# Second mixer's projections in a fixed order, modulation chunks one per weight block and six of them in the attention

## The chip, the cores and the metric

One core of one Trainium2 chip runs the kernel. The metric is the device time of one execution in microseconds (us). TensorE does matrix products, VectorE and GpSimd elementwise work, ScalarE activation functions and copies; SyncE (SP) issues most of the DMA transfers. Each engine takes its instructions in the order in which the program lists them for it, and waits for others by semaphores.

## What is computed

A backbone of two layers. Each layer is a token mixer and a mixture of experts, both behind an RMS norm that is modulated by six vectors made from a condition `c`. Layer 0's mixer is a recurrence; layer 1's, which the change touches, is a bidirectional chunkwise mLSTM over 256 context and 512 latent tokens. Cut to that:

```python
def adaln(cond, w, b):
    m = jax.nn.silu(cond) @ w + b          # 1024 -> 6 * 1024
    return jnp.split(m, N_MOD, axis=-1)    # shift, scale, gate; shift, scale, gate

# layer 1
hx = modulate(rms_norm(x, g1), sh1, sc1)
p = hx @ w_in                              # q 512, k 512, v 1024, o 1024, gates 32 columns
...
w_intra = jnp.exp(log_w - m_t[..., None])
s = jnp.einsum('bhtd,bhsd->bhts', qc, kc) * w_intra
num = w_inter[..., None] * jnp.einsum('bhtd,bhde->bhte', qc, c_mat) + jnp.einsum('bhts,bhse->bhte', s, vc)
den = w_inter * jnp.einsum('bhtd,bhd->bht', qc, n_vec) + jnp.sum(s, axis=-1)
h_out = num / jnp.maximum(jnp.abs(den), jnp.exp(-m_t))[..., None]
...
y = (rms_norm_per_head(h_f + h_b) * sigmoid(o)) @ w_out
x = x + gt1 * y
x = x + gt2 * hier_moe(modulate(rms_norm(x, g2), sh2, sc2))
```

## The kernel before

Three stages of layer 1 matter here: the projections (`ml_in`), the attention (`ml_att`), and the product with `w_out` and the experts behind them.

**Projections.** `w_in` is taken in blocks of 256 columns. A block is loaded as fp32 (1 MB, tile `ws`, L1667) into a pool of three slots, and split into a high and a low part: ScalarE writes `whi` (L306), GpSimd `wlo` (L309), each in two halves of four k-tiles. A job is then one PSUM tile of 24 matmuls: eight k-tiles by three products of high and low parts. Blocks 0 and 1 are q, 2 and 3 are k, 4 to 7 are v, 8 to 11 are the output gate. q and k are made channel-major (`chan`, L1684, 512 tokens a matmul), k's context, v and the output gate token-major (`toks`, L1692, 256 columns a matmul). ScalarE copies each finished tile out of PSUM (qT L1755 and L1776, kT L1778, kc L1783, v L1789, og L1796). The PSUM pool `pa` of these tiles has two buffers. Block 0 and the gates are made ahead, during the norm.

**Modulation chunks.** Layer 1's modulation is 24 chunks of 256 columns, numbered n = 4 v + q for vector v and quarter q. Chunks 8 to 23 are made here, `ada_vec` (L194): a load of 1 MB into a slot of the same pool (L168), eight products on VectorE that sum over k-tiles with c as scalar (L202 the first, L204 seven more, tile `vpart`), and later a finish: two matmuls with ones (L210, four records in the trace), a VectorE add into `modT` (L214), a multiplication by the norm's weight where v is 1 or 4 (L218), and at q = 3 of v = 2, 3, 4 a transpose into a row (L227). Two chunks are begun in each of blocks 1 to 8 and finished at the end of the block after.

**Gates.** `ml_gates` makes the exponents of the chunkwise form: a chain on VectorE (L1819 to L1838, scans among it) with two activations between, then 18 exponentials on ScalarE (L1840 to L1848). `tokens`, called at block 3, transposes them. `ml_queries` (L1886), called at block 9, spreads the decays by matmuls (L1898) and weights q.

**What sets the order.** Ahead of this stretch the order is written out by hand. Within it a scheduler decides, instruction by instruction, from dependences and estimated times; the program order above is only its input. The attention is again in a hand-written order: eight steps, each with the scores and weights of the next step, states, and `values` of its own, two PSUM tiles `po` per step (`b0` 0 and 2). VectorE turns each tile into `hs` in six steps (L1993 to L2001). Behind the last transposes come the matmuls with `w_out` (L801), whose weights use the same three slots.

Of the kernel before, what the change touches and what calls it, by code (L numbers as in the profile page):

```python
# [17 lines left out]
P = 128  # L18
# [84 lines left out]
class Net:  # L103
# [90 lines left out]
    def ada_vec(self, l, n, pool, psum, work, tag="pg", m=2):  # L194


        V = self.nc.vector
        w = self.ada_load(l, n, pool)
        v, q = divmod(n, 4)
        part = work.tile([P, m, 256], F32, name="vpart", bufs=4 if m == 1 else 1)  # L200
        for i in range(m):
            V.tensor_scalar(part[:, i], w[:, 0, :], self.cT[:, 0, i:i + 1], None, op0=OP.mult)  # L202
            for k in range(1, KD):
                V.scalar_tensor_tensor(part[:, i], w[:, k, :], self.cT[:, k, i:i + 1], part[:, i],  # L204
                                       op0=OP.mult, op1=OP.add)
        def finish():
            ps = psum.tile([P, 512], F32, name=tag)
            for i in range(m):
                for b in range(2):
                    self.nc.tensor.matmul(ps[:, 2 * i + b:2 * i + b + 1], part[:, i, b * P:(b + 1) * P], self.ones,  # L210
                                          start=True, stop=True)
            ks = slice(2 * q, 2 * q + 2)
            o = self.modT[:, l, v, 0:m, ks]
            V.tensor_add(o, ps[:, 0:2 * m].rearrange("p (i b) -> p i b", b=2),  # L214
                         self.adab[l][:, v, ks].unsqueeze(1).to_broadcast([P, m, 2]))
            if v in (1, 4):
                g = (self.g1T if v == 1 else self.g2T)[l][:, ks]
                V.tensor_mul(o, o, g.unsqueeze(1).to_broadcast([P, m, 2]))  # L218
            if q == 3 and v >= 2 and (l, v) != (1, 5):
                self.ada_rows(l, v, ps[:, 256:512], work, m)  # L220
        return finish
# [1422 lines left out]
    def ml_in(self, x, xcp, wsp):  # L1644
# [4 lines left out]
        with ExitStack() as st:  # L1649
# [103 lines left out]
            nc.gpsimd.memset(self.v1[:, :, :, 128:129], 1.0)  # L1753
            for c in range(2):
                nc.scalar.activation(self.qT[:, c, :], psq[:, c * 512:(c + 1) * 512], AF.Copy, scale=0.125)  # L1755
            ps = psg
            for q in range(4):
                dst = (self.li, self.lf)[q % 2][32 * (q // 2):32 * (q // 2) + 32, :]
                nc.scalar.activation(dst, ps[32 * q:32 * q + 32, 256:1024], AF.Identity, bias=bg[32 * q:32 * q + 32, :])
            tokens = self.ml_gates(sp, gp, pb)  # L1760

            ada = []
            for i in range(12):
                parts = parts1 if i == 1 else split(load(256 * i, 256)) if i else None
                last, ada = ada, []
                if 1 <= i <= 8:
                    ada = [self.ada_vec(1, 6 + 2 * i + j, wsp, pb, sp, m=1) for j in range(2)]
                if i == 0:
                    pass
                elif i < 4:  # L1770
                    for c in range(2):
                        blk = 2 * (i % 2) + c
                        ps = pa.tile([P, 1024], F32, name="pa")[:, 0:512]
                        chan(ps, parts, c, CTX, NTOK)
                        if i < 2:
                            nc.scalar.activation(self.qT[:, blk, :], ps, AF.Copy, scale=0.125)  # L1776
                        else:
                            nc.scalar.activation(self.kT[:, blk, :], ps, AF.Copy)  # L1778
                    if i >= 2:
                        for t in range(2):  # L1780
                            ps = pa.tile([P, 1024], F32, name="pa")[:, 0:256]
                            toks(ps, parts, t)
                            nc.scalar.activation(self.kc[:, t, 256 * (i - 2):256 * (i - 1)], ps, AF.Copy)  # L1783
                elif i < 8:
                    for t in range(NT0):
                        ps = pa.tile([P, 1024], F32, name="pa")[:, 0:256]
                        toks(ps, parts, t)
                        h = 2 * (i - 4)
                        nc.scalar.activation(self.v1[:, t, h:h + 2, 0:128],  # L1789
                                             ps.rearrange("p (h e) -> p h e", e=128), AF.Copy)  # L1790
                else:
                    for t in range(4):
                        ps = pa.tile([P, 1024], F32, name="pa")[:, 0:256]
                        toks(ps, parts, 2 + t)
                        c = slice(256 * (i - 8), 256 * (i - 7))
                        nc.scalar.activation(self.og[:, t, c], ps, AF.Sigmoid)  # L1796
                if i == 3:
                    tokens()
                    gates.__exit__(None, None, None)
                if i == 7:  # L1800
                    hcp.__exit__(None, None, None)
                if i == 9:
                    self.ml_queries(store.enter_context(tc.tile_pool(name="queries", bufs=1)), pb)
                for f in last:
                    f()
        return store

    def ml_gates(self, sp, gp, psum):
# [31 lines left out]
        nc.scalar.activation(emn, m[:, CTX:NTOK], AF.Exp, scale=-1.0)  # L1840
        for d, (a, z) in enumerate(dirs):
            for c, (s, e) in enumerate(chunks):
                end = e - 1 if d == 0 else s
                if c > 0:
                    prev = s - 1 if d == 0 else (e if c < 4 else 0)
                    nc.scalar.activation(win[a:z, s - CTX:e - CTX], g[a:z, s:e], AF.Exp, bias=m[a:z, prev:prev + 1])
                if c == 0 or c != (4 if d == 0 else 1):
                    nc.scalar.activation(wst[a:z, s:e], r[a:z, s:e], AF.Exp, bias=g[a:z, end:end + 1])  # L1848
# [35 lines left out]
        return tokens  # L1884

    def ml_queries(self, pool, psum):  # L1886

        nc, V = self.nc, self.nc.vector
        self.qw = pool.tile([P, 2, 4, SEQ], F32, name="qw")
        self.dec = pool.tile([P, 2, 4, 4], F32, name="dec")  # L1890
        for d in range(2):
            for b in range(0, 4, 2):
                pw = psum.tile([P, 1024], F32, name="pg").rearrange("p (a n) -> p a n", a=2)
                for c in range(2):
                    sel = pool.tile([64, 2, 64], F32R, name="sel", bufs=2)
                    h = 2 * (b + c)
                    V.tensor_copy(sel, self.both[:, d, h:h + 2].bitcast(F32).unsqueeze(2).to_broadcast([64, 2, 64]))
                    nc.tensor.matmul(pw[:, c, :], sel.rearrange("p a b -> p (a b)"), self.wr, start=True, stop=True)  # L1898
                V.tensor_mul(self.qw[:, d, b:b + 2, :], self.qT[:, b:b + 2, :], pw)
                o = P - 1 if d == 0 else 0  # L1900
                V.tensor_copy(self.dec[:, d, b:b + 2, :], pw[:, :, o:512:P])

    def ml_att(self, st, yT):
# [69 lines left out]
        def weigh(c, h0, d):  # L1973
            V.tensor_mul(pds[c, h0][d], pds[c, h0][d], pss[c, h0])

        def values(i, between=None):
# [5 lines left out]
            for b0 in (0, 2):  # L1982
# [19 lines left out]
                if b0 == 0 and between:  # L2002
                    between()
# [44 lines left out]
        with tc.manual_schedule(engines={ET.PE, ET.DVE, ET.Activation, ET.Pool}):  # L2048
# [19 lines left out]
            for i in range(8):  # L2068
                nxt = steps[i + 1] if i < 7 else None
                if nxt:  # L2070
                    scores(*nxt)
                    weigh(*nxt, 0)
                if i < 3:
                    state(0, i + 1)
                if i:
                    squares(i - 1, G)
                    if i % 2 == 0:
                        roots(i // 2 - 1, 0, 8)
                    if i == 7:
                        roots(3, 0, 4)  # L2080
                if nxt:
                    weigh(*nxt, 1)
                values(i, (lambda: scale(3, 0, 4)) if i == 7 else None)
# [11 lines left out]
def body(tc, A, out, upto=None, dbg=None):  # L2095
    nc = tc.nc
    with ExitStack() as ctx:
# [34 lines left out]
        with ExitStack() as st:  # L2132
            n.ml_att(st, yT)
# [43 lines left out]
```

## Times and profile before

| what | us |
| --- | --- |
| three runs | 1878.0, 1901.58, 1873.12 |
| median | 1878.0 |
| profiled execution, its own time | 1875.53 |
| span of the profiled execution | 1873.5 |
| TensorE busy | 1736.0 (93%) |
| VectorE busy | 941.6 (50%) |
| ScalarE busy | 543.3 (29%) |
| GpSimd busy | 390.4 (21%) |

The profile is of one execution. Its page gives the busy time of every engine and the span in 40 equal slices; the trace can be asked for the busy time in any stretch, for what an engine waited for, and for the instructions one by one, with their start, duration and the idle time before them with what ended it. The mean granted TensorE clock of the execution is 0.964 of full speed. Neighbouring instructions of one kind are drawn together into one row with a count; matmuls are pipelined, so their durations overlap and the distance of starts tells the pace.

### The profile page before, as it was taken

The numbers are of one execution on the slowest core, as the hardware profiler recorded it, in microseconds if no ns is written. First come the engines' busy times: TensorE is split into PE (matmuls) and PEld (weight loads), VectorE is DVE, ScalarE is ACT, GpSimd is POOL, SyncE is SP. The second block draws the span as 40 slices with busy tenths as digits, with TensorE's granted clock in tenths as the row PEclk, the third lists the DMA queues.
The fourth block names the chain that finished last, engine by engine and source line by source line (L and its number), as shares of the span: only waits on it lengthen the run. The fifth ranks groups of instructions, "written<-read, shape, count | busy, mean of one in ns | idle before, by whom it ended". The sixth has DMA issues, their size and how long they took to land. (4 is left out here: it accounts for less than half of the span.)

```text
span 1873.5 us, 26159 instructions
## 1 busy us (share of the span) xinstructions
PE 1736.0 (93%) x10181; PEld 1038.1 (55%) x10181; DVE 941.6 (50%) x1877; ACT 543.3 (29%) x1007; POOL 390.4 (21%) x303
## 2 busy tenths in 40 slices
PE   7999998997999999999988998999978999999996
PEld 5777776685443434344447898977653444444342
DVE  5477776656444464545455743156552333333234
ACT  5367775422111110111126312145421111111112
POOL 3433322402111010101025242221221111111111
PEclk9999998998999999999999998999989999999999
DMA  9544432555999989999942545200869999999995
GB/s 331 178 157 149 126 120 90 177 174 227 416 419 418 371 315 419 418 419 419 418 161 80 180 135 164 84 1 1 311 244 418 421 421 420 420 420 420 420 421 222
DMA packets 158240, 521.13 MB, mean 278 GB/s; under 512 B 16744, under 2 KB 93806, under 8 KB 109984
## 3 DMA queue, kind: packets, MB, share of 16 engines
q1 hardware_dynamic: 151344, 497.08, 68.6%
q0 software_dynamic: 6768, 22.33, 3.0%
q8 instruction: 82, 1.34, 0.3%
q14 instruction: 46, 0.38, 0.1%
HBM read 518.59 MB, written 7.39 MB: 281 GB/s over the span
## 5 line engine op out<-in xcount | busy, mean ns | idle before, releaser
L1214 DVE TENSOR_TENSOR xl<-xl,ps 128x512 f32<-128x512 f32 x136 | 87.7, 684 | 296.6 <-PE ps L1212 296.6
L1198 POOL DMA_INDIRECT xg<-h_rows,idx x32 | 38.4, 1199 | 567.1 <-DVE slot L1181 257.1
L1276 PE MATMUL pd<-wring,hT 128*64 128x512 f32 (+1 forms) x616 | 152.1, 610 | 2.7 <-ACT hT L1268 2.1
L1251 PE MATMUL pu<-wring,xT 128*64 128x512 f32 (+1 forms) x576 | 149.1, 610 | 0.4 <-DMA wring<-in_l_moe_w_up_dram 0.4
L309 POOL TENSOR_TENSOR wlo<-ws,whi 128x1024 fp32r<-128x1024 f32 x41 | 114.4, 2800 | 119.6 <-ACT whi L306 118.1
L1239 POOL TENSOR_TENSOR yl<-yw,yh 128x512 fp32r<-128x512 f32 x60 | 76.4, 1273 | 248.7 <-ACT yh L1238 246.6
L1251 PE MATMUL pg<-wring,xT 128*64 128x512 f32 (+1 forms) x576 | 127.7, 594 | 0.0
L1258 ACT ACTIVATE sg<-pg 128x512 f32<-128x512 f32 x32 | 19.1, 597 | 351.0 <-PE pg L1251 351.0
L1692 PE MATMUL pa<-whi,hhi 128*128 128x256 f32 x352 | 103.6, 294 | 10.9 <-ACT v L1789 9.1
L1238 ACT ACTIVATE yh<-yw 128x512 fp32r<-128x512 f32 x64 | 40.3, 630 | 250.1 <-DVE yw L1235 127.5
L1230 DVE SCALAR_TENSOR_TENSOR yw<-pd,slotr,gt2b 128x512 f32<-128x512 f32 x62 | 46.5, 751 | 119.2 <-PE pd L1276 119.1
L1692 PE MATMUL pa<-whi,hlo 128*128 128x256 f32 x352 | 102.6, 292 | 0.0
L1692 PE MATMUL pa<-wlo,hhi 128*128 128x256 f32 x352 | 102.2, 290 | 0.0
L1251 PE MATMUL pu<-yt,xT 128*64 128x512 f32 (+1 forms) x408 | 95.6, 596 | 0.2 <-DMA yt<-in_l_moe_w_up_dram 0.2
L1276 PE MATMUL pd<-yt,hT 128*64 128x512 f32 (+1 forms) x376 | 86.9, 595 | 1.6 <-ACT hT L1268 1.1
L1207 ACT ACTIVATE xT<-tr 128x512 f32<-128x512 f32 x64 | 35.1, 595 | 179.5 <-PE tr L1206 179.5
L1276 PEld LDWEIGHTS pd<-wring,hT 128*64 128x64 f32 (+1 forms) x616 | 44.5, 133 | 75.3 <-issue 69.4
L1214 DVE TENSOR_TENSOR xl<-xl,pd 128x512 f32<-128x512 f32 x128 | 82.1, 680 | 0.3 <-PE pd L1212 0.3
L1251 PEld LDWEIGHTS pu<-wring,xT 128*64 128x64 f32 (+1 forms) x576 | 40.7, 133 | 73.8 <-issue 69.7
L1251 PE MATMUL pg<-yt,xT 128*64 128x512 f32 (+1 forms) x400 | 81.4, 596 | 0.0
L1212 PE MATMUL ps<-yh,oht 128*128 128x512 f32 x166 | 75.0, 452 | 5.9 <-DVEq L1355 5.9
L1251 PEld LDWEIGHTS pg<-wring,xT 128*64 128x64 f32 (+1 forms) x576 | 38.5, 131 | 70.9 <-issue 68.6
(628 smaller groups left out, 3924.8 us busy)
## 6 DMA issues: line engine op xcount, KB each, us to landing
wring<-in_l_moe_w_gate_dram SPq DMA_DIRECT2D x62, 1024.0 KB
wring<-in_l_moe_w_up_dram SPq DMA_DIRECT2D x61, 1024.0 KB
wring<-in_l_moe_w_down_dram SPq DMA_DIRECT2D x59, 1024.0 KB
yt<-in_l_moe_w_up_dram SPq DMA_DIRECT2D x41, 1024.0 KB
ws<-in_l_ada_w_dram SPq DMA_DIRECT2D x40, 1024.0 KB
yt<-in_l_moe_w_gate_dram SPq DMA_DIRECT2D x39, 1024.0 KB
yt<-in_l_moe_w_down_dram SPq DMA_DIRECT2D x35, 1024.0 KB
ws<-in_l_moe_w_gate_dram SPq DMA_DIRECT2D x24, 1024.0 KB
```

What stands on the lines that cost most here:

```text
L309: eng_lo.tensor_sub(lo, x, hi.bitcast(F32))
L1198: nc.gpsimd.indirect_dma_start(out=xg, out_offset=None, in_=hd, in_offset=bass.IndirectOffsetOnAxis(ap=idx[:, 0:1], axis=0), bounds_check= ...
L1207: nc.scalar.activation(xT[:, 4 * h:4 * h + 4, :], pt[:, :, 0:n], AF.Copy)
L1212: nc.tensor.matmul(ps, lhsT, y, start=i == 0, stop=i == len(ys) - 1)
L1214: V.tensor_add(xs, xs, ps)
L1230: V.scalar_tensor_tensor(y[k], ps, r[:, 1:2], g[:, 0, :], op0=OP.mult, op1=OP.mult)
L1238: nc.scalar.activation(yh, y, AF.Copy)
L1239: eng.tensor_sub(yl, y, yh.bitcast(F32))
L1251: nc.tensor.matmul(ps[a:a + w, :], xT[:, 4 * h + j, a:a + w], pieces[n, e[i], h][:, j, :], start=h == 0 and j == 0, stop=h == 1 and j == 3)
L1258: nc.scalar.activation(s, pg, AF.Silu)
L1276: nc.tensor.matmul(pd[a:a + w, :], hT[:, 2 * h + j, a:a + w], ring.down(2 * p + i, h, j, c), start=h == 0 and j == 0, stop=h == 1 and j == 1)
L1692: nc.tensor.matmul(ps, h, w[:, k % 4, :], start=k == 0 and j == 0, stop=k == KD - 1 and j == 2)
```

## The change

The whole stretch of the projections is put under a hand-written order, on SyncE too. Raw blocks are loaded two ahead; the next block's split is made in two halves ahead of a block's first two jobs; one chunk per block is begun in blocks 1 to 10 (chunks 8 to 17), its products behind the block's first job, its finish behind the first job of the block after. Chunks 18 to 23 go into the attention: their products are dealt out three, two and two at a time over the steps, a finish at the end of six steps, in free columns of the tile `po`. The exponentials are issued behind block 3's second job, `tokens` behind block 4's third, the queries in four pieces in blocks 9 and 10, with four `sel` tiles instead of two. qT's copies stand ahead of those of the gates.

```diff
@@ ada_vec becomes ada_prods (the eight products) and ada_fin
+        for b in range(2):
+            self.nc.tensor.matmul(ps[:, b:b + 1], part[:, b * P:(b + 1) * P], self.ones, start=True, stop=True)
+        ks = slice(2 * q, 2 * q + 2)
+        o = self.modT[:, l, v, 0, ks]
+        V.tensor_add(o, ps[:, 0:2], self.adab[l][:, v, ks])
+        if v in (1, 4):
+            V.tensor_mul(o, o, (self.g1T if v == 1 else self.g2T)[l][:, ks])
+        if q == 3 and v >= 2 and (l, v) != (1, 5):
+            self.ada_rows(l, v, ps[:, 8:136], work, 1)
@@ ml_in
+            st.enter_context(tc.manual_schedule(engines={ET.PE, ET.DVE, ET.Activation, ET.Pool, ET.SP}))
+            raws, ada, part = {2: load(512, 256)}, {}, {}
...
+            chunk(1)
+            fetch(3)
...
-            for i in range(12):
-                parts = parts1 if i == 1 else split(load(256 * i, 256)) if i else None
-                last, ada = ada, []
-                if 1 <= i <= 8:
-                    ada = [self.ada_vec(1, 6 + 2 * i + j, wsp, pb, sp, m=1) for j in range(2)]
...
+            for i in range(1, 12):
...
+                if i in ada:
+                    part[i] = sp.tile([P, 256], F32, name="vpart", bufs=2)
+                    prods = self.ada_prods(7 + i, ada.pop(i), part[i])
+                for j, job in enumerate(jobs):
+                    if j < 2 and i < 11:
+                        new += split(raws[i + 1], halves=(j,))
+                    job()
+                    if j == 0 and i - 1 in part:
+                        finish(i - 1)
+                    if j == 0:
+                        for f in prods:
+                            f()
+                        chunk(i + 1)
+                        fetch(i + 3)
+                    if i == 3 and j == 1:
+                        exps()
+                    if i == 4 and j == 2:
+                        tokens()
+                        gates.__exit__(None, None, None)
+                    if i == 8 and j == 1:
+                        queries = self.ml_queries(store.enter_context(tc.tile_pool(name="queries", bufs=1)), pb)
+                    if i in (9, 10) and j in (0, 2):
+                        queries.pop(0)()
...
+            self.chunks = [(n, self.ada_load(1, n, wsp)) for n in (18, 19, 20)]
@@ ml_att: behind each tile po; ada_some(3) and ada_some(2) also behind the two weighings of a step
-                if b0 == 0 and between:
-                    between()
+                if b0 == 0:
+                    ada_some(2)
+                    if between:
+                        between()
+                else:
+                    ada_end(po[:, 1, 376:512])
```

Three places of the order show what moves. The first is VectorE at the gates: L1819 to L1837 before are L1839 to L1857 after, and the products are L202 and L204 before, L199 and L201 after. Before, rows in their order:

```order
L1819 SCALAR_TENSOR_TENSOR og<-lf 64x768
L204 SCALAR_TENSOR_TENSOR vpart<-ws,cT,vpart 128x256 x6
L1821 TENSOR_SCALAR og<-og 64x768
L204 SCALAR_TENSOR_TENSOR vpart<-ws,cT,vpart 128x256 x3
L1823 SCALAR_TENSOR_TENSOR lf<-lf,og 64x768
L204 SCALAR_TENSOR_TENSOR vpart<-ws,cT,vpart 128x256
L1830 SCALAR_TENSOR_TENSOR og<-lf,li 32x768
```

After, the end of the same chain and what stands behind it (L212 is the add of a finish):

```order
L1856 TENSOR_TENSOR li<-li,og 64x768
L1857 TENSOR_TENSOR lf<-og 64x768
L1858 MEMSET og 64x768
L199 TENSOR_SCALAR vpart<-ws,cT 128x256
L201 SCALAR_TENSOR_TENSOR vpart<-ws,cT,vpart 128x256 x7
L212 TENSOR_TENSOR modT<-pg,svm_136 128x2
```

The products of a chunk stood between the gates' steps and now stand behind all of them. The second place is TensorE at the end of block 2's first job (L1679 is `chan` after the change, L209 a finish): here the finish of the first chunk stands.

```order
L1679 MATMUL pa<-hhi_8112,whi 128x512
L1679 MATMUL pa<-hlo_8113,whi 128x512
L1679 MATMUL pa<-hhi_8112,wlo 128x512
L209 MATMUL pg<-ones,vpart 128x1 x2
L1679 MATMUL pa<-hhi_8112,whi 128x512
```

Before, the first finish stood at the end of block 2, for two chunks at once, ahead of block 3's jobs:

```order
L1692 MATMUL pa<-whi,hhi_8110 128x256
L1692 MATMUL pa<-whi,hlo_8111 128x256
L1692 MATMUL pa<-wlo,hhi_8110 128x256
L210 MATMUL pg<-ones,vpart 128x1 x4
L1684 MATMUL pa<-hhi_8112,whi 128x512
```

It has moved forward by one channel job and two token jobs. The third place is TensorE in the attention behind the values of step 2 (counted from 0), where chunk 19 is finished (L209) and its row is transposed (L222), ahead of the next step's scores (L1994, L1998):

```order
L2028 MATMUL po<-v_8399,w_10383 128x129
L2029 MATMUL po<-C,qw 128x129
L209 MATMUL po<-ones,ws 128x1 x2
L222 MATMUL po<-ident,modT 8x128
L1994 LDWEIGHTS identb
L1994 MATMUL pw<-mask,identb 128x512
L1998 MATMUL pw<-gr,both 128x128 x4
```

Before the change the scores followed the values directly.

## Rows read from the trace of the kernel before

**Rows 1.** Busy by windows; columns as in the first line, clock in shares.
```profile
core 0: us, PE busy (x) PEld busy (x) DVE busy (x) ACT busy (x) POOL busy (x), PEclk, DMA share, GB/s
1023.90:1218.40 194.50, 179.42 (x1289) 169.60 (x1289) 88.28 (x197) 51.54 (x93) 56.93 (x21) 0.96 0.44 141
1218.40:1308.20 89.80, 88.69 (x596) 65.50 (x595) 54.17 (x158) 44.91 (x155) 16.91 (x14) 1.00 0.00 1
1500.00:1600.00 100.00, 97.71 (x490) 40.85 (x489) 33.57 (x74) 14.51 (x31) 15.93 (x12) 1.00 1.01 420
...
1143.00:1145.00 2.00, 2.00 (x12) 2.00 (x11) 0.00 (x0) 0.00 (x0) 2.00 (x2) 0.50 0.00 0
```

**Rows 2.** Waits of TensorE from 1020 to 1225: us, times, longest.
```profile
PE pa L1692 <- ACT v L1789: 9.1, 2, 5.0
PE pg L227 <- DVE modT L218: 2.9, 1, 2.9
```

**Rows 3.** Timeline, ScalarE: start, us, instruction, [idle before, what ended it].
```profile
1059.75 2.01 ACT L306 ACTIVATE whi<-ws 128x1024 fp32r<-128x1024 f32 x2 [5.46 <-DMA ws<-in_l_ml_w_in_dram]
```

**Rows 4.** Timeline of TensorE in the projections.
```profile
1023.97 0.50 PE L1684 MATMUL pa<-hhi,whi 128*128 128x512 f32 x1 [1.66 <-ACT qT L1755]
...
1045.66 0.39 PE L1684 MATMUL pa<-hhi,wlo 128*128 128x512 f32 x1
...
1142.43 0.41 PE L1692 MATMUL pa<-whi,hlo 128*128 128x256 f32 x1
...
1144.99 0.41 PE L1692 MATMUL pa<-whi,hlo 128*128 128x256 f32 x1
...
1158.78 0.58 PE L210 MATMUL pg<-ones,vpart 128*128 128x1 f32 x4
1159.23 0.36 PE L1692 MATMUL pa<-whi,hhi 128*128 128x256 f32 x1
...
1195.90 0.73 PE L1898 MATMUL pg<-wr,sel 64*128 64x512 f32 x2
...
1199.73 0.28 PE L1692 MATMUL pa<-whi,hlo 128*128 128x256 f32 x1
...
1218.19 0.28 PE L1692 MATMUL pa<-wlo,hhi 128*128 128x256 f32 x1
```

**Rows 5.** Timeline of ScalarE around the gates.
```profile
1022.84 1.08 ACT L1755 ACTIVATE qT<-pa 128x512 f32<-128x512 f32 x2
...
1024.85 0.90 ACT L1759 ACTIVATE lf<-pa,bg 32x768 f32<-32x768 f32 x1
...
1035.82 1.28 ACT L1840 ACT_TABLE_LOAD   x1
1041.54 0.63 ACT L1840 ACTIVATE og<-og 64x512 f32<-64x512 f32 x1 [4.43 <-DVE lf L1837]
...
1047.21 0.60 ACT L1778 ACTIVATE kT<-pa 128x512 f32<-128x512 f32 x1
```

**Rows 6.** Timeline of VectorE in the projections.
```profile
1022.86 0.70 DVE L1838 MEMSET og<- 64x768 f32 x1
...
1025.78 0.95 DVE L1819 SCALAR_TENSOR_TENSOR og<-lf 64x768 f32<-64x768 f32 x1 [0.46 <-ACT lf L1759]
...
1116.70 5.61 DVE L204 SCALAR_TENSOR_TENSOR vpart<-ws,cT,vpart 128x256 f32<-128x256 f32 x14
...
1160.56 2.50 DVE L202 TENSOR_SCALAR vpart<-ws,cT 128x256 f32<-128x256 f32 x1
...
1163.05 0.34 DVE L202 TENSOR_SCALAR vpart<-ws,cT 128x256 f32<-128x256 f32 x1
```

**Rows 7.** Timeline of GpSimd in the projections.
```profile
1116.71 10.21 POOL L309 TENSOR_TENSOR wlo<-ws,whi 128x1024 fp32r<-128x1024 f32 x2 [12.51 <-ACT whi L306]
...
1158.25 4.66 POOL L309 TENSOR_TENSOR wlo<-ws,whi 128x1024 fp32r<-128x1024 f32 x2 [12.57 <-ACT whi L306]
```

**Rows 8.** Timeline of VectorE in the attention: first and last step of one tile.
```profile
1262.88 0.16 DVE L1993 SCALAR_TENSOR_TENSOR den<-po,eT 128x4 f32<-128x4 f32 x1 [1.35 <-PE po L1990]
...
1264.51 0.35 DVE L2001 SCALAR_TENSOR_TENSOR hs<-po,den,hs 128x128 f32<-128x128 f32 x1
```

More of the change, by code (lines that the diff above doesn't have):

```diff
@@ L192, in ada_sum, with ada_prods @@
             nc.vector.tensor_mul(o, o, g.unsqueeze(1).to_broadcast([P, 2, m]))
-    def ada_vec(self, l, n, pool, psum, work, tag="pg", m=2):
+    def ada_prods(self, n, w, part):
         V = self.nc.vector
-        w = self.ada_load(l, n, pool)
-        v, q = divmod(n, 4)
[L200 to L221, printed above, removed]
@@ new lines, in ada_prods, with ada_fin @@
+        c = self.cT[:, :, 0:1]
+        steps = [lambda: V.tensor_scalar(part, w[:, 0, :], c[:, 0], None, op0=OP.mult)]
+        for k in range(1, KD):
+            steps.append(lambda k=k: V.scalar_tensor_tensor(part, w[:, k, :], c[:, k], part, op0=OP.mult, op1=OP.add))
+        return steps
+    def ada_fin(self, l, n, part, ps, work):
+        V = self.nc.vector
+        v, q = divmod(n, 4)
+        for b in range(2):
[7 more added lines that the diff above has]
+            self.ada_rows(l, v, ps[:, 8:136], work, 1)
@@ new lines, in finish @@
+            def finish(i):
+                self.ada_fin(1, 7 + i, part.pop(i), pb.tile([P, 1024], F32, name="pg"), sp)
+            parts, queries = parts1, []
+            for i in range(1, 12):
+                jobs = [lambda c=c: channels(i, parts, c) for c in range(2 if i < 4 else 0)]
+                if i > 1:
+                    jobs += [lambda t=t: tokens_of(i, parts, t) for t in
+                             (range(2) if i < 4 else range(NT0) if i < 8 else range(2, NT0))]
+                new, prods = [], []
+                if i in ada:
[21 more added lines that the diff above has]
+                        queries.pop(0)()
@@ L1800, in ml_in @@
                 if i == 7:
                     hcp.__exit__(None, None, None)
[L1802 to L1805, printed above, removed]
+                parts = new
+            self.chunks = [(n, self.ada_load(1, n, wsp)) for n in (18, 19, 20)]
         return store
@@ L1890, in ml_queries, with select, selects, step @@
         self.dec = pool.tile([P, 2, 4, 4], F32, name="dec")
[L1891 to L1903 removed]
+        sels = {}
+        def select(h, d):
+            sels[d, h] = pool.tile([64, 2, 64], F32R, name="sel", bufs=4)
+            V.tensor_copy(sels[d, h], self.both[:, d, h:h + 2].bitcast(F32).unsqueeze(2).to_broadcast([64, 2, 64]))
+        todo = [(d, b) for d in range(2) for b in range(0, 4, 2)]
+        def selects(n):
+            if n < len(todo):
+                for c in range(2):
+                    select(2 * (todo[n][1] + c), todo[n][0])
+        def step(n):
+            d, b = todo[n]
+            pw = psum.tile([P, 1024], F32, name="pg").rearrange("p (a n) -> p a n", a=2)
+            for c in range(2):
+                nc.tensor.matmul(pw[:, c, :], sels[d, 2 * (b + c)].rearrange("p a b -> p (a b)"), self.wr,
+                                 start=True, stop=True)
+            selects(n + 2)
+            V.tensor_mul(self.qw[:, d, b:b + 2, :], self.qT[:, b:b + 2, :], pw)
+            o = P - 1 if d == 0 else 0
+            V.tensor_copy(self.dec[:, d, b:b + 2, :], pw[:, :, o:512:P])
+        selects(0)
+        selects(1)
+        return [lambda n=n: step(n) for n in range(len(todo))]
+    def ml_att(self, st, yT, wsp):
         tc, nc = self.tc, self.nc
@@ L2001, in values, with ada_some, ada_end @@
                     V.scalar_tensor_tensor(o, po[:, j, 129:257], den[:, j, 1:2], o, op0=OP.mult, op1=OP.add)
-                if b0 == 0 and between:
-                    between()
+                if b0 == 0:
+                    ada_some(2)
+                    if between:
+                        between()
+                else:
+                    ada_end(po[:, 1, 376:512])
+        chunks, prods, done = self.chunks, [], []
+        def ada_some(n):
+            for _ in range(n):
+                if not prods and chunks:
+                    c, w = chunks.pop(0)
+                    prods.extend(self.ada_prods(c, w, w[:, 0, :]))
+                    prods.append((c, w))
+                if prods:
+                    prods.pop(0)()
+                if prods and isinstance(prods[0], tuple):
+                    done.append(prods.pop(0))
+        def ada_end(ps):
+            if done:
+                c, w = done.pop(0)
+                self.ada_fin(1, c, w[:, 0, :], ps, w1)
+                if c + 3 < 24:
+                    chunks.append((c + 3, self.ada_load(1, c + 3, wsp)))
         def squares(i, eng):
```

85 lines of the change are left out of this document (39 added, 46 removed).

## The prediction, with its working

> **What bounds the kernel now.** The profiled execution took 1875.53 us, 2.0 of them around its span. The change touches layer 1's mixer, so I read three stretches of the table by windows [rows 1]. From 1023.90 to 1218.40 (the projections) TensorE is busy 179.4 of 194.5 us, VectorE 88, ScalarE 52, GpSimd 57, and the DMA engines less than half: TensorE sets the pace, and only its idle time is to be had. From 1218.40 to 1308.20 (the attention) TensorE is busy 88.7 of 89.8 at full clock, VectorE 54, and nothing is loaded. Behind it stands the second expert stage, with DMA share 1.01 and 420 GB/s; its weights start only when the attention has given its memory back, so it moves with the attention's end and passes a shift on one for one.
>
> Next, what TensorE waits for in the projections [rows 2]: 9.1 us in two waits named after ScalarE's v copies, and 2.9 for the modulation row. The two long ones end when a weight block's split has been made from a load that landed late: the load of block 3 shows its price, ScalarE stood 5.46 us for it [rows 3].
>
> Then the pitch, from first and last start of an undisturbed run [rows 4]. Channel-major: 96 matmuls from 1023.97 to 1045.66, 95 intervals, 0.2283 us each. Token-major: 1199.73 to 1218.19, 154 intervals, 0.1199 each. A job is 24 matmuls, 5.48 or 2.88 us. After the wait of 5.0 the matmuls stand at 0.213 instead of 0.12 (1142.43 to 1144.99, 12 intervals), and the granted clock of 1143 to 1145 is 0.50, the level of 1.2 GHz [rows 1, 4]. So a long wait costs twice; that one cost about 1.9 us more behind it.
>
> The stretch from 1023.97 to 1218.3 is 194.3. Six channel jobs and 44 token jobs are 6 x 5.48 + 44 x 2.88 = 159.5. Sixteen finishes of 0.45 for two chunk matmuls each (1158.78 to 1159.23 for four records, [rows 4]) are 7.2. The queries' eight matmuls are 3.0 (0.73 for two). What is left is 24.6: the waits, the low clock behind them, and some 1.7 of token transposes, which stay.
>
> **Removed.** The two late loads go (9.1 us and about 3.3 of low clock): raw blocks now come two blocks ahead, a block lasts 11.5 to 22 us of TensorE, and one load takes some 5.4 [rows 3]. With one chunk per block, SP issues 2 MB per block where it issued 3. I take no wait for any block from 4 on. The kT wait goes in its old place, since the 18 exponentials no longer stand in front of that copy. The row wait of 2.9 goes to the attention (chunk 19, below). The queries' wait for `sel` goes, because the four tiles are made a block earlier.
>
> **Added or moved, in TensorE's time from a start at 1023.6** (qT's copies are first on ScalarE now; q's last matmul ends at 1023.97 - 1.66 = 1022.3, and two copies take 1.08, [rows 4, 5]):
>
> 1. Jobs 159.5, token transposes 1.7, queries 3.0.
> 2. Ten finishes of 0.45: 4.5. Six chunks move out.
> 3. Two row transposes (chunks 11 and 15) now stand on TensorE right behind their finish. They wait for one VectorE add: nearest row a VectorE step on four columns, 0.16 us [rows 8]; with the way there and back I estimate 1.0 each, 2.0. Bounds: nothing (0.3 for the transpose) and the 2.9 that one such wait cost [rows 2].
> 4. Chunk 1's finish, the main doubt. The order shows the eight products of chunk 1 behind the whole gates chain, and TensorE takes the finish after three channel jobs, at 1023.6 + 72 x 0.2283 = 1040.0. The chain ran from 1025.78 to 1041.5 before [rows 5, 6], with eleven products in it, which cost it some 1.4 us by the gaps that they filled late (estimate). It now starts at about 1027.1, since four copies of 0.9 stand behind qT's on ScalarE, and so ends at 1027.1 + 15.7 - 1.4 = 1041.4. Behind it: a memset of 0.7 [rows 6], the first product (0.34 alone, but 2.50 where it stood beside GpSimd's lower half, [rows 6, 7]), and seven of 0.40 (14 took 5.61). That is 1045.2 without and 1047.4 with the collision: a wait of 5.2 to 7.4. GpSimd makes block 3's first lower half just then, so I take 7.4. Queued behind the finish on TensorE is all of block 2; nothing else can go past it. Low clock behind it as after the wait of 5.0: 2.0. Together 9.4; bounds 0 (rows hidden) and what rival C says.
> 5. The exponentials, moved behind the copies of block 3's second job: kT copy 0.6 to 0.8, table 1.28, 18 rows from 1041.54 to 1047.2, then the next copy 0.4, in all 8.2 us [rows 5]. TensorE has two token jobs to do meanwhile (5.76) before it lacks a bank: 2.4, and 0.8 for the clock (bounds 0 and 1.6). Together 3.2; bounds 0 and 4.
>
> Sum: 159.5 + 1.7 + 3.0 + 4.5 + 2.0 + 9.4 + 3.2 = 183.3, so the projections end at 1206.9 instead of 1218.3: 11.4 earlier.
>
> **Given back in the attention.** The six finishes are 6 x 0.45 = 2.7 of a full TensorE. The 48 products (some 20 us) fit into VectorE's 35.6 idle ones. Chunk 19 has its add, its multiplication and its transpose with TensorE waiting, and VectorE first owes the six steps from `den` to `hs` of that tile: 1262.88 to 1264.86, 2.0 us [rows 8], then 0.16 and 0.15: about 2.4, and 0.5 for clock and fills. That is 5.6. Bounds: 3.0 (that wait hidden) and 9 (two more finishes hold a VectorE queue up by their products). Chunks 21 to 23 are loaded in slots that chunks 18 to 20 free; the output weights' first load has two steps of 11 us for its 5.4, hidden.
>
> Net -11.4 + 5.6 = -5.8 on 1875.5: **1869.7 us**. The median of the runs shown, 1878.0, is 2.5 above the profiled execution, and the runs spread from 1873 to 1902; I forecast on the profiled one's scale.
>
> **The page's rule on VectorE and GpSimd.** Rows first: a product's first step took 2.50 beside GpSimd's lower half of 4.66 and 0.34 without it, but 14 products that started together with two lower halves (1116.70, 10.21 us on GpSimd) took 5.61, nothing lost; GpSimd's halves took twice their 4.66 instead [rows 6, 7]. The Trainium skill's "GPSIMD Engine Reference", section Key points, says that GpSimd shares its SBUF interfaces with VectorE and contends with VectorE instructions in a 2-port mode or with two SBUF inputs. By that rule the gates' scans, sums and products would contend too, not only the first step; the trace agrees for the first step, and for the products only in that GpSimd's side was longer. This rule is what rival C would be made of.
>
> **Rivals.**
>
> A. The forecast, 1869.7: chance 0.57, its own range 1862 to 1877.
>
> B. The new order hides more than I give it: gates chain shorter without the products between, chunk 1's products done by 1040, exponentials in time. Steps 4 and 5 return 12.6 and the transposes 1: about 1856. For it: VectorE is at 45% in that stretch. Against: products behind the gates in the order, with only 16.4 us of TensorE work ahead of the finish. 0.2.
>
> C. The other side, slower than before. GpSimd's lower halves of blocks 2 and 3, issued ahead of the jobs 1,0 to 2,1, now run beside the gates chain. A half is 2.3 us alone and up to 5.1 in contention (4.66 and 10.21 for two). If three of them hold the chain for their length, it is 7 to 15 us later: 1876.7 to 1885, say 1880. It decides when chunk 1's finish waits over 7.4 + 5.8 = 13.2 us. For it: the 2.50 row. Against: the 14 products of 5.61. 0.14.
>
> D. The change doesn't do what it says: with three slots the raw loads still wait for products and splits, and the blocks stay late. 12 us of the gain go: 1877 to 1882. Against: a slot is freed a block ahead of its load's use. 0.05.
>
> E. The shift is swallowed by the DMA-bound stage behind: 1875. Against: the loads there start behind the attention. 0.04.
>
> **How the numbers follow.** The likeliest case gives 1869.7. To leave out at most 2 in 10, the range goes down to B's centre and up to C's: 1856 to 1881. Faster or slower by over 2% (about what a measurement of this kernel can tell from no change) would be 37 us either way, more than all of TensorE's idle time in the projections gives (24.6), and more than C's upper end: 0.03 and 0.03; the same 0.94.
>
> **What would show it.** Right: no wait at token-major blocks for a split; one wait of 5 to 8 us at the finish behind the third channel job, released by VectorE, with clock 0.50 behind it; a wait of 2 to 3 us at block 4's start behind the exponentials; in the attention one wait of 2 to 3 us at the row transpose of chunk 19; the attention starting 11 us earlier and ending 6 earlier, the rest unchanged in length. Wrong: waits of TensorE for ScalarE's splits after a late load (D), a first wait over 13 us (C) or none (B), or an expert stage that is longer by what the mixer saved (E).

## The result and the profile after

The changed kernel takes 1926.7 us (median of 4, 1920.0 to 1928.0) against 1875.6 for the kernel before (median of 4): ratio 1.0265, interval 1.0233 to 1.0298. It is 51 us slower; 1869.7 was forecast. (The interval leaves out executions over 1.5% above the fastest of their kernel, which here are those with the lowest mean clock, so below medians and ranges of all executions are given beside it.)

The page of the changed kernel: its span, and the granted clock in 40 slices of 48 us.

```profile
span 1925.0 us, 26158 instructions
...
PEclk9999999998999999999988999955988999999998
```

Two slices at half clock lie in the attention; before, no slice was below 8. The table by windows, columns as in [rows 1]: projections, the attention up to its step 1, from step 1 to its end, the first matmuls behind that, and the expert stage.

```profile
1021.20:1211.50 190.30, 172.54 (x1264) 162.69 (x1264) 88.36 (x143) 55.00 (x97) 52.70 (x23) 0.96 0.35 111
1211.50:1245.00 33.50, 32.40 (x278) 25.14 (x277) 25.37 (x66) 12.19 (x38) 9.38 (x8) 1.00 0.01 1
1246.50:1346.00 99.50, 89.75 (x303) 64.46 (x303) 43.60 (x126) 31.39 (x108) 6.28 (x5) 0.50 0.16 53
1354.00:1358.00 4.00, 4.00 (x21) 2.78 (x20) 2.14 (x7) 0.00 (x0) 0.00 (x0) 1.00 0.68 232
1550.00:1650.00 100.00, 97.75 (x491) 40.34 (x488) 33.09 (x72) 14.51 (x31) 15.96 (x12) 1.00 1.01 420
```

What TensorE waited for from 1000 to 1400 (us, times, longest), the counterpart of [rows 2]:

```profile
PE pg L209 <- DVE vpart L201: 13.3, 1, 13.3
PE po L209 <- DVE hs L2040: 10.4, 5, 2.1
...
PE pa L1687 <- ACT kc L1782: 2.3, 1, 2.3
PE pa L1679 <- POOL wlo L304: 1.2, 1, 1.2
...
PE pg L222 <- DVE modT L212: 0.5, 2, 0.3
```

The late splits, the row wait of 2.9 and the `sel` wait are gone, as the change means them to be. The projections take 190.7 us from their first job to the attention's first transpose, instead of 195.0: 4.3 won. The attention, from there to the first load of the expert stage, takes 151.4 instead of 92.2: 59.2 lost. (Ahead of it all the program was 2.7 us earlier; over the runs below, of either order, that start scatters from 1016.5 to 1025.7.) The expert stage is as before.

Where the attention's clock goes, on TensorE's timeline (start, us, instruction, [idle before]):

```profile
1244.93 0.49 PE L2029 MATMUL po<-C,qw 64*128 64x129 f32 x2
1247.49 1.01 PE L209 MATMUL po<-ones,ws 128*128 128x1 f32 x4 [2.08 <-DVE hs L2040]
1248.37 0.59 PE L1994 MATMUL pw<-mask,identb 128*128 128x512 bf16 x1
...
1255.25 0.80 PE L2028 MATMUL po<-v,w 128*128 128x129 f32 x2
...
1346.33 7.28 PE L796 MATMUL po<-ws,yT 128*128 128x512 f32 x10
...
1353.81 0.47 PE L2028 MATMUL po<-v,w 128*128 128x129 f32 x2
```

A finish waits 2.08 us, not at chunk 19 alone but at five of six: its two matmuls write the tile `po`, and VectorE must first have read `po` for `hs`. In the first of these waits the granted clock falls to 0.50 (the level of 1.2 GHz), and the pair of 129-column matmuls that took 0.42 from start to start takes 0.73. The clock comes back 106 us later, while ten matmuls of 512 columns (L796) run. The steps between hold matmuls of 512 columns too (L1994, bf16, one or two in a step), and it stayed down through them.

The gates chain on VectorE, and GpSimd beside it:

```profile
1024.79 0.95 DVE L1839 SCALAR_TENSOR_TENSOR og<-lf 64x768 f32<-64x768 f32 x1 [8.87 <-ACT lf L1765]
...
1031.80 8.37 DVE L1853 TENSOR_TENSOR_SCAN og<-og,lf 32x256 f32<-32x256 f32 x5
...
1042.10 4.01 DVE L1853 TENSOR_TENSOR_SCAN og<-og,lf 32x256 f32<-32x256 f32 x5
...
1047.02 0.94 DVE L1857 TENSOR_TENSOR lf<-og 64x768 f32<-64x768 f32 x1
...
1048.95 3.61 DVE L201 SCALAR_TENSOR_TENSOR vpart<-ws,cT,vpart 128x256 f32<-128x256 f32 x7
```

```profile
1030.04 9.23 POOL L304 TENSOR_TENSOR wlo<-ws,whi 128x1024 fp32r<-128x1024 f32 x3 [9.65 <-ACT whi L301]
1041.14 3.17 POOL L304 TENSOR_TENSOR wlo<-ws,whi 128x1024 fp32r<-128x1024 f32 x1 [1.87 <-issue]
```

The chain takes 23.2 us (1024.79 to 1047.96) instead of the 14.3 of the sum, and the finish behind it waits 13.3. Of the ten scans of L1853, four take 2.5 to 2.8 us, one for each of the four halves; the other six share the rest.

The products behind block 3's first job, and the half beside them:

```profile
1073.53 5.62 DVE L201 SCALAR_TENSOR_TENSOR vpart<-ws,cT,vpart 128x256 f32<-128x256 f32 x7
```

```profile
1074.36 2.42 POOL L304 TENSOR_TENSOR wlo<-ws,whi 128x1024 fp32r<-128x1024 f32 x1 [3.29 <-ACT whi L301]
```

Seven products take 5.62 us here and 3.61 at 1048.95, where GpSimd stands still; this half takes 2.42, no longer than one alone.

### The profile page after: what moved, and what is told of

Its sections match the earlier page's. It is cut to its first block, busy times and chain, and to the rows that moved or that the text cites. A ratio compares the mean times of both kernels' runs of the same rounds, so it can differ in the third digit from the quotient of the medians.

```text
span 1925.0 us, 26158 instructions
## 1 busy us (share of the span) xinstructions
PE 1774.1 (92%) x10181; PEld 1063.3 (55%) x10181; DVE 959.5 (50%) x1877; ACT 543.7 (28%) x1007; POOL 382.6 (20%) x303
## 5 line engine op out<-in xcount | busy, mean ns | idle before, releaser
L304 POOL TENSOR_TENSOR wlo<-ws,whi 128x1024 fp32r<-128x1024 f32 x41 | 106.4, 2598 | 124.0 <-ACT whi L301 120.6
```

The lines of the kernel that those rows point to most:

```text
L304: eng_lo.tensor_sub(lo, x, hi.bitcast(F32))
```

## Experiments

The first runs put three theories of the attention against each other. W: a wait for VectorE lets the clock fall, and it stays low. R: the short matmuls of the finishes, or the products on VectorE, keep it down by themselves. N: a wait costs its own length and a few us of low clock, as in the projections. Two more came later. H: what comes ahead does it, the projections that now run without pauses. E: the attention stands at the edge by itself, and what the change adds to it tips it.

**Finishes in a tile of their own.** The edit, in `values` and in `ada_end`:

```diff
-                    ada_end(po[:, 1, 376:512])
+                    ada_end()
...
+                ps = pps.tile([P, 4, P], F32, name="ps").rearrange("p a b -> p (a b)")
```

> The changed kernel, with the six finishes of the attention in a PSUM tile of their own (a score tile that is free by then) instead of the free columns of po. Its row of chunk 19 still stands behind the finish. Theory W (a finish that writes po must wait until VectorE has read po, and the clock that falls in that wait does not come back within the attention): five waits of 2.1 us for hs go, but TensorE still waits some 2.5 us for chunk 19's add in step 2, the clock falls there, one step later than before: one step of some 8 us and 10 us of waits saved, about 1908. Theory R (the short matmuls of the finishes or the products on VectorE keep the clock down by themselves): clock 0.50 from step 1 on, only the 10 us of waits go, about 1916. Theory N (a single wait costs its own length and a few us of low clock, as in the projections): about 1875.

Measured: 1914.3 us (5 executions, 1912.0 to 1928.0; the kernel before, 13 on the same chip, 1879.1). The five waits are gone, and one of 1.4 for chunk 19's add is left, in step 2. But in the profiled execution the clock had fallen in the scores behind step 0, ahead of any finish and any wait (eight matmuls of the scores, 1.10 us at full clock):

```profile
1232.76 1.52 PE L2008 MATMUL ps<-qT,kT 64*128 64x128 f32 x8
```

All three theories miss the place; R has the time (1916).

**The row later as well.** Chunk 19's transpose is kept in `row` and issued behind the next step's scores:

```diff
+                if row:
+                    row.pop()()
```

> As the own tile, and chunk 19's row transpose is issued behind the next step's scores and products instead of right behind its finish, so that TensorE waits for VectorE nowhere in the attention. Theory W: granted clock 1.00 through the attention, its length 92 plus the finishes' 3 us, 56 us less than in the changed kernel: about 1871. Theory R: clock 0.50 still, about 1914.

Measured: 1917.7 (4 executions, 1902.8 to 1922.8). Theory W falls: no wait is needed. R, with 1914, holds here. TensorE waits for nothing from step 0 on, and the clock falls all the same, here beside the first finish. TensorE's timeline, and the windows ahead of and behind it:

```profile
1243.44 0.61 PE L209 MATMUL ps<-ones,ws 128*128 128x1 f32 x4
...
1244.30 1.11 PE L1998 MATMUL pw<-gr,both 64*128 64x128 f32 x4
...
1250.66 0.80 PE L2028 MATMUL po<-v,w 128*128 128x129 f32 x2
```

```profile
1210.00:1243.00 33.00, 32.27 (x276) 25.03 (x276) 25.01 (x66) 11.84 (x38) 9.13 (x8) 1.00 0.00 1
1245.00:1340.00 95.00, 95.00 (x313) 68.86 (x314) 47.81 (x135) 32.44 (x113) 7.52 (x6) 0.50 0.21 67
```

TensorE is busy for 95.00 of 95.00 us, at half clock throughout. Busy time does not bring the clock back here.

**One wait in the kernel before.** The same place, without any chunk moved:

```diff
+                if b0 == 2 and i == 1:
+                    for c2 in range(2):
+                        nc.tensor.matmul(po[:, 1, 376 + c2:377 + c2], self.ident, self.ones, start=True, stop=True)
```

> The kernel before, with two matmuls of 128x1 into the free columns of po at the end of step 1 of the attention alone (their result is not used), so that TensorE waits there once for VectorE's six steps on po. No chunk is moved. Theory W, a clock that stays low once it has fallen: one wait of 2.1 us and clock 0.50 from there until the w_out matmuls, some 45 us more, about 1920. If every wait costs only its own length and a few us behind it: 2.1 + 2 to 8, at most 1886. Theory R (the products or the number of finishes): about 1878.

Measured: ten executions from 1886.8 to 1929.8, median 1913.6: 8 to 51 us over the median of the kernel before, nine of them 18 or more. (The interval's ratio is 1.0095, 1.0050 to 1.0141.) In the profiled execution the clock fell about 1 us behind that wait and came back 102 us later:

```profile
1254.07 0.61 PE L2004 MATMUL po<-ones,ident 128*128 128x1 f32 x4 [2.08 <-DVE hs L2001]
...
1255.61 2.01 PE L1969 MATMUL ps<-qT,kT 64*128 64x128 f32 x8
```

So no chunk, no product and no fixed order is needed, and N falls. The edit adds the wait and two short matmuls together; the next run has the short matmuls alone.

**Six finishes without a wait in the kernel before.** As the last, in steps 1 to 6, into a free score tile:

```diff
+                if b0 == 2 and 1 <= i <= 6:
+                    ps = pps.tile([P, 4, P], F32, name="ps").rearrange("p a b -> p (a b)")
+                    for c2 in range(2):
+                        nc.tensor.matmul(ps[:, c2:c2 + 1], self.ident, self.ones, start=True, stop=True)
```

> The kernel before with two matmuls of 128x1 at the end of each of steps 1 to 6 of the attention, into a score tile that is free by then, so that TensorE waits for nothing (the results are not used); no chunk is moved. Theory E: 0.45 us a step in which TensorE streams next to no columns is enough, the clock falls in step 1 or 2 in most executions: about 1915. If only a wait tips it: 1878 + 2.7 = 1880. Theory H: 1880 too, since the projections are those of before.

Measured: 1920.6 (4 executions, 1906.0 to 1924.2; before, 13 executions, 1883.4). Twelve matmuls of one column, 2.7 us in all, cost some 37 us. From step 1 on:

```profile
1248.00:1348.00 100.00, 99.94 (x323) 70.68 (x323) 34.17 (x105) 32.16 (x113) 6.39 (x6) 0.50 0.00 1
```

In this execution it fell some 2 us behind the first pair. The projections are those of before, so H is not needed, and neither are the products of R: its short matmuls are enough, without a wait. What the wait of the run above added to its own two is not shown.

**All sixteen chunks in the projections.** The other way round: the new order ahead, the attention of before.

```diff
+            keys = sorted([(i, 0) for i in range(1, 11)] + [(i, 1) for i in range(2, 8)])
+            nums = {k: 8 + n for n, k in enumerate(keys)}
...
-            self.chunks = [(n, self.ada_load(1, n, wsp)) for n in (18, 19, 20)]
+            self.chunks = []
```

> The changed kernel's fixed order with all sixteen chunks in the projections (one in each of blocks 1 to 10, a second one in blocks 2 to 7), chunk 1's finish in block 3, the exponentials behind block 3's first job; TensorE's work in the attention is that of the kernel before. Theory E (the attention stands at the edge of falling to the low clock, and what the change adds to it tips it): clock 1.00 through the attention as before, projections about 170 us from first job to last instead of 194: 1850 to 1858. Theory H (it is what comes ahead, the projections without pauses, that lets the clock fall in the attention): clock 0.50 there again, 1895 to 1905.

Measured: 1875.0 (11 executions, 9 of them 1869.0 to 1880.1, two 1902.4 and 1914.7), ratio 0.9957 (0.9924 to 0.9990) against 1883.4. H falls: the order ahead is the change's, and the attention mostly keeps its clock. In two executions it fell, the profiled one among them (at 1262, in step 3). The kernel before does the same: of 71 executions beside these experiments, 54 lie from 1868 to 1890 and 17 from 1890 to 1919, the long ones with a lower mean clock (0.938 in that of 1919.5, 0.964 in that of 1869.6). No trace of a long one was kept, so that its clock falls in the attention is inferred. The 20 us that I expected in the projections did not come. The waits say why:

```profile
PE pg L1887 <- DVE sT L1889: 7.1, 1, 7.1
...
PE pg L209 <- DVE modT L212: 3.4, 1, 3.4
PE pg L209 <- DVE vpart L201: 1.3, 1, 1.3
```

With two chunks in a block, TensorE reaches the token transposes and block 2's finishes while VectorE is still at sixteen products.

**Columns beside the finishes.** Own tile and later row as above, and ahead of each finish:

```diff
+                for f in range(3):
+                    nc.tensor.matmul(ps, self.identb, self.mask[:, 0, :].unsqueeze(1).to_broadcast([P, 4, P]),
+                                     start=True, stop=True)
```

> The kernel with the finishes in their own tile and chunk 19's row later (1917.7 us, no wait of TensorE in the attention, clock 0.50 from step 1's end), plus three matmuls of 128x512 ahead of each finish, whose result is overwritten. Theory E: with columns streamed beside the finishes the clock holds: 1874 + 6 x 0.7 = about 1872 to 1880. Theory H: it falls as before, about 1922.

Measured: 1904.7 (4 executions, 1902.4 to 1905.7), 13 us better at the median than without (1902.8 to 1922.8). In the profiled execution the clock held until step 4 and fell some 2.5 us behind a wait that my edit had made: the score tile held step 3's transposes, and ScalarE had not yet copied them out.

```profile
1268.40 1.16 PE L2008 MATMUL ps<-qT,kT 64*128 64x128 f32 x8 [1.02 <-ACT yT L2108]
...
1271.50 0.80 PE L2028 MATMUL po<-v,w 128*128 128x129 f32 x2
```

Half a hit: the added matmuls keep the clock up longer, but not through the attention. That the wait undid it is argued from this one trace.

**GpSimd away from the gates.** Blocks 2 and 3 without their lower halves:

```diff
+                    elif j < 2 and i <= 2:
+                        hi = wk.tile([P, 4, 256], F32R, name="whi")
+                        nc.scalar.activation(hi, raws[i + 1][:, 4 * j:4 * j + 4, :], AF.Copy)
+                        new.append((hi, parts1[j][1]))
```

> The changed kernel without the lower halves of blocks 2 and 3 on GpSimd: their upper halves are copied alone, and the matmuls read block 1's lower halves in their place, so the k columns are not the reference's. GpSimd then stands still beside the gates chain. If GpSimd's work stretched the scans: the scans return to 0.3 us each, the chain is 8 us shorter, the wait of 13.3 at chunk 1's finish falls to 4 to 6, the projections are 8 to 9 us shorter: about 1917. If the order behind the copies stretched the chain: wait still 12 to 13, 1926.

Measured: the scans on VectorE, and the finish on TensorE:

```profile
1030.01 1.91 DVE L1857 TENSOR_TENSOR_SCAN og<-og,lf 32x256 f32<-32x256 f32 x5
...
1033.85 1.92 DVE L1857 TENSOR_TENSOR_SCAN og<-og,lf 32x256 f32<-32x256 f32 x5
```

```profile
1042.36 0.99 PE L209 MATMUL pg<-ones,vpart 128*128 128x1 f32 x4 [6.29 <-DVE vpart L201]
```

The same ten scans take 3.8 us instead of 12.4, the chain 14.6 instead of 23.2, the wait 6.3 instead of 13.3, the projections 181.8 instead of 190.7. So GpSimd's halves alone stretched the chain. (The whole, 1913.3, still has the low clock of the attention.)

**Chunk 1's finish one block later.**

```diff
-                    if j == 0 and i - 1 in part:
-                        finish(i - 1)
+                    if j == 0 and i != 2:
+                        for k in [k for k in part if k < i]:
+                            finish(k)
```

> The changed kernel, with chunk 1's finish issued one block later, ahead of chunk 2's, so that TensorE does not reach it before its products are done; the split on GpSimd beside the gates chain is as in the changed kernel. If the 13.3 us wait is paid by the finish alone: wait and its low clock go, 13.3 + 5, about 1908. If the late gates chain only makes the next thing late (chunk 2's products, the exponentials at block 3): half of it comes back as a wait at block 3 or 4, about 1917.

Measured: 1911.3 (5 executions, 1907.6 to 1919.6), projections 181.4 instead of 190.7. Of 13.3 us of wait, 4.2 come back at block 3, for chunk 2's products; the low clock behind it comes back too. Between the two expectations.

**A kernel that beats both.** Two attempts put things later. First all finishes behind a block's third job and the token transposes behind block 4's sixth; then the same with two matmuls of 512 columns at the end of steps 0 to 6, which nothing reads:

```diff
+                elif i < 7:
+                    ps = pps.tile([P, 4, P], F32, name="ps")
+                    for f in range(2):
+                        nc.tensor.matmul(ps, self.identb, self.mask[:, 0, :].unsqueeze(1).to_broadcast([P, 4, P]),
+                                         start=True, stop=True)
```

> All sixteen chunks in the projections (1875.0 us, with waits of 7.1, 3.4 and 1.3 us and low clock behind them), but each block's finishes behind its third job instead of its first, and the token transposes behind block 4's sixth job instead of its third, so that VectorE's products are done by then. Theory E: TensorE is left with the 1.2 us waits at the start, the attention starts some 14 us earlier than there and is as before: 1856 to 1862, with single executions some 20 to 40 us longer where the clock falls, as with the kernel before. If the waits only move to the next step that needs VectorE: 1870 to 1875.

> The same with two matmuls of 128x512 at the end of steps 0 to 6 of the attention, into a free score tile that nothing reads. Theory E: 7 x 0.45 = 3.2 us more work, and the clock falls in fewer executions: median 1859 to 1866, the longest not over 1875. If columns beside the steps' ends do not matter: the same scatter as without them, 3 us later.

Measured: 1895.5 (12 executions, 1882.4 to 1909.6) and 1880.5 (12, 1874.4 to 1884.5). Both miss their forecasts. They have a new wait, which puts even the shortest executions of the first at 1882: the finish's add now stands behind the products on VectorE, and the row transposes on TensorE wait for it.

```profile
PE pg L222 <- DVE modT L212: 12.0, 2, 7.3
PE pa L1687 <- ACT kT L1778: 4.7, 2, 2.8
```

Against each other they are the cleanest test of theory E: the projections are alike (199.4 and 199.9 us in the profiled executions), the second has 3 us more work in the attention, and its median is 15 us lower. Seven of the first's twelve executions lie over 1891, none of the second's; the range shrinks from 27 us to 10.

So the last kernel has the finishes behind each block's first job again, block 2's two alone later, the exponentials in two halves, and the 512-column matmuls:

```diff
+                    if i == 3 and j == 2:
+                        finish((2, 0))
+                        finish((2, 1))
...
+                    if i == 3 and j in (0, 2):
+                        for f in exps[:9] if j == 0 else exps[9:]:
+                            f()
...
-                    if i == 4 and j == 2:
+                    if i == 4 and j == 5:
```

> All sixteen chunks in the projections with the finishes behind each block's first job, except block 2's two (behind block 3's third job), the exponentials in two halves (behind block 3's first and third job), the token transposes behind block 4's sixth, and two matmuls of 128x512 at the end of steps 0 to 6 of the attention. Theory E: no wait of TensorE over 2 us in the projections, attention some 14 us earlier than before, clock held in the attention: 1860 to 1867 in all executions. If VectorE's queue makes a new wait (a row transpose behind products): 1868 to 1875.

> The kernel before with the same two matmuls of 128x512 at the end of steps 0 to 6 of the attention and nothing else. Theory E: 3.2 us more work, and the scatter of the kernel before (1870 to 1919) goes, since it comes from the clock falling in the attention in some executions: median about 1876, longest under 1882. If the scatter of before has another cause: median and longest both 3 us up.

Measured: **1862.8** (11 executions, 1857.9 to 1869.1) against 1882.3 (22 executions, 1868.1 to 1916.4): ratio 0.9905, interval 0.9876 to 0.9935, about 1% and clear of no change. The median lies in the forecast range, the ends 2 us outside it. Projections and attention:

```profile
1020.00:1202.70 182.70, 174.37 (x1289) 164.85 (x1289) 113.20 (x200) 55.60 (x98) 51.76 (x24) 0.99 0.47 150
1203.00:1296.00 93.00, 92.19 (x610) 67.09 (x611) 54.49 (x162) 44.66 (x155) 16.73 (x14) 1.00 0.00 1
```

The projections take 182.2 instead of 195.0, with sixteen finishes in them, and the attention 95.1 instead of 92.2. The kernel before with the fillers alone: 1883.3 (12 executions, 1876.7 to 1890.8) against the same 1882.3, ratio 1.0014 (0.9987 to 1.0040). Beside the kernel before its median does not move, and none of its executions is over 1891 (5 of the 22 are, and 16 of all 71); twelve executions alone would be too few to say so. Median and longest are 7 and 9 us over what I expected, so two fillers a step do not hold the clock always (in the profiled execution it was down for 10 us, and came back 3 us behind the next pair). Set beside the six finishes without a wait, in the same place and tile, the runs differ by 37 us at the median: 1920.6 with six pairs of one column in fp32, 1883.3 with seven of 512 columns in bf16. Whether the columns or the type make the difference no run tells.

## Why the prediction was wrong

**What bounds the kernel** was read rightly: TensorE, with the expert stage moving along one for one (100 us of it look alike before and after).

**Removed** came as forecast: no wait for a late block, the `sel` wait gone.

**Step 3** (two row transposes, 2.0) was too high: their waits are 0.5 in all. **Step 5** (exponentials, 2.4 and 0.8) measured 2.3 and no low clock behind it.

**Step 4** was mis-sized. I shortened the chain of before and looked for the collision only at the first product behind it. GpSimd's halves of blocks 2 and 3 stood beside the scans: 8.6 us more (12.4 against 3.8). The wait was 13.3 instead of 7.4; what I had called rival C, with the deciding point of 13.2. I had weighed it down by the 14 products that lost nothing beside two halves. That read one side of the row only: the two halves took 5.55 us longer than a pair alone (10.21 against 4.66), almost the 5.61 of the products, so GpSimd stood still for them [rows 6, 7]. After the change VectorE is the one that stands still, with four scans of the chain and with the products (5.62 against 3.61). What decides which of the two waits no run here shows. The rule of the Trainium skill's "GPSIMD Engine Reference", section Key points, is that GpSimd and VectorE contend over instructions with two SBUF inputs. The run without lower halves agrees for the scans (3.8 us instead of 12.4). A term of the sum was also low: seven products that each add to the same sum take 3.61 us here, 0.52 each; 0.40 had been read where two chunks' products ran together. (The range of 11.5 to 22 us for a block was wrong as well: by the prices of a job it is 11.0 to 17.3. Nothing hung on it.)

With all that the projections were still 4.3 us shorter than before, against 11.4 forecast. With 5.6 given back in the attention the kernel would have been 1.3 us slower than before, as rival C had it for a wait just over 13.2: a time within 2%.

**Given back in the attention** is the step that decided: 5.6 forecast with bounds 3 to 9, measured 59.2. It failed twice. I let only chunk 19 wait for VectorE, because the finishes write free columns of `po`; the trace shows each of five waiting 2.08 us for the reads of the same tile. And I took the clock as in the projections, where it is back a few us behind a wait (0.213 instead of 0.12 for some 4 us, [rows 4]). In the attention it came back only with the ten matmuls of `w_out`, 106 us later. The full clock of 1.00 over 89.8 us in [rows 1] I read as a property of the stretch; it is one of two ways in which the stretch can run. No rival had that. That the change could make the long way the usual one was nowhere in the sum. The range of the three runs shown, 1873 to 1902, was the hint: the profile showed only an execution of the short kind.

How the 59.2 divide between the waits and the clock is seen from two runs: with own tile and later row, no wait and the clock down from step 1 on, the attention took 139.7, so low clock and finishes cost 47.5 and the waits the rest, about 12 (10.8 of it is idle time named in the trace).

**What stays open:** why the clock fell in step 0 in the run with an own tile, where TensorE had done nothing that the kernel before doesn't do. The executions of the kernel before fall too, and by their times mostly later (most of the long ones are 13 to 31 us over the others; the profiled run with one wait, where it fell at step 1's end, was 46 over). Open too is what it is in the added matmuls that tips or holds the clock. The runs show what makes the fall more likely, not where it comes.

## What to carry to other kernels

Before work is moved into a stretch at full clock, look at whether all executions of the kernel run it so: if single runs are some per cent longer with a lower mean clock, the stretch may stand at the edge, and 0.45 us of one-column matmuls per 10 us cost 37 us here. A matmul that writes free columns of a PSUM tile waited here for the readers of the other columns; a tile of its own took that wait away, though not the low clock. And before a VectorE chain is put beside GpSimd's elementwise work, read both engines' rows: where one lost nothing, the other had stood still for about as long, and in the new order it can be the other way round.

## What was not expected of the hardware

- TensorE at granted clock 0.50 for 95 us in which it was busy throughout (95.00 of 95.00), on fp32 matmuls of 129 columns and fewer with nine bf16 ones of 512 among them. In another pair of kernels two more of 512 columns per step took 15 us off the median.
- Five scans of 32x128 to 32x256 took 8.37 us beside GpSimd's halves of 3.1 us and 1.91 without them; seven products took 5.62 beside a half and 3.61 alone.
- Fourteen products lost nothing beside two halves; it was the halves that took 10.21 us instead of 4.66.
